# An expert kernel whose gate-times-gelu weights are formed by ScalarE, with VectorE only spreading the gates

## The chip, the core and the metric

The kernel runs on one core of a Trainium2 chip. A core has five engines that work side by side, each through its own queue and in that queue's order: TensorE (PE in the profile) multiplies matrices, VectorE (DVE) does elementwise arithmetic and reductions, ScalarE (ACT) computes functions and copies with a scale, GpSimd (POOL) here only issues gathers, and SyncE (SP) issues plain loads. Data comes from HBM by DMA. The metric is the device time of one execution in microseconds (us), as the median of several.

## The reference

One layer of a decoder block: three token mixers, gates and an output projection, and then a mixture of experts (PEER) in which each of 1024 tokens picks 16 experts in each of 8 heads out of 16384. The change touches only this last part:

```python
top_s, pos = lax.top_k(cand, PEER_TOPK)
idx = jnp.take_along_axis(cand_idx, pos, axis=-1)
gate = jax.nn.softmax(top_s, axis=-1)

def chunk(args):
    hc, ic, gc = args
    act = jax.nn.gelu(jnp.einsum('chkd,cd->chk', u[ic], hc).astype(jnp.float32), approximate=False)
    w = (gc * act).astype(h.dtype)
    return jnp.einsum('chk,chkd->cd', w, v[ic])
```

For each token, 128 rows of `u` are gathered and multiplied with the token's row, gelu of the product times the gate is the expert's weight, and the weighted sum of 128 rows of `v` is the output.

## The kernel before

The 1024 tokens are eight blocks of 128. Two blocks (`DENSE`, line 31) are computed against all 16384 experts with plain matmuls. The other six go by gathers, and these are the **sets** of the change. A set (`g`, 32 to a block, 192 in all) is four tokens with their 128 experts, in four gathers of 128 rows of `u` and four of `v`, 512 KB each. Partition p of a gather belongs to token p // 32 of the set.

`Experts.step` (line 1133) is one gather, i = 0 to 3 within the set. It does in this order: at i = 0 it takes the set's tokens `hb`, spread over the partitions (`spread_rows`, line 1080: two matmuls on PE into `pb`, two copies on ScalarE into `hb`; written two gathers ahead, at i = 2 of the set before); then it runs what is due of earlier sets (`run_behind`, line 1148); issues the gather of `v` (line 1097 by `fetch`); and on VectorE multiplies the gathered `u` with `hb` and sums over the row (line 1151) into column i of `parts`. After i = 3 the rest of the set is put in `behind`, in three parts that run one gather apart, each at the `run_behind` of the next set's gathers:

1. at the next set's i = 0: `gelu`, one ScalarE instruction on `parts` (128 x 4), into `gel`. ScalarE's other functions need another table, so most gelus are framed by two table loads.
2. at i = 1: `weights`, two VectorE instructions: `gel` times the gates `gT` (line 1165), and its product with the constant `spread` (line 1166), which puts each weight in its token's column of a 128 x 32 matrix, four of them in `wz`.
3. at i = 2: `sums` (line 1177), 16 matmuls (32 in the profile) that multiply `wz` with the four `v` into `po`. VectorE adds `po` to the output row after every eighth set.

Gathered rows live in rings of buffers: five for `u` and six for `v` (`UP, VP`, line 44). A gather of `u` waits until the dot product has read its buffer, a gather of `v` until the sums have; both stand in one queue on GpSimd. `wz`, `gel`, `parts` and `hb` come from a pool with two buffers each (line 82).

The sets run beside all other work, the **filler**: attention and projections of the three token groups (2, 3 and 3 blocks; the sets begin once the first group's experts are chosen), then the dense blocks. A planner in the loop at the end of the kernel (lines 1428 to 1433) interleaves the two in the order of writing by its own estimates of matrix and DMA time. Line 90 then fixes ScalarE's order: its instructions stand in its queue as they are written. On all other engines a scheduler of the framework orders the instructions, by the place at which they are written and by a model of when their inputs are ready. So a step that is written later on ScalarE moves there by exactly that, and the others' queues are rearranged around it.

The names of tiles in the profile are those of the code; `bank` is a PSUM tile of the filler, `big` and `wide` are activations, `w` weights, `e` a projection's result on its way, `sc` expert scores, `sp` a bfloat16 copy of the normalised tokens on its way to DRAM (`b3d`).

Of the kernel before, what the change touches and what calls it, by code (L numbers as in the profile page):

```python
# [7 lines left out]
F32 = mybir.dt.float32  # L8
# [3 lines left out]
AF = mybir.ActivationFunctionType  # L12
# [65 lines left out]
def block_kernel(ctx: ExitStack, tc: tile.TileContext, io):  # L78
    nc = tc.nc
    pool = lambda name, bufs, **kw: ctx.enter_context(tc.tile_pool(name=name, bufs=bufs, **kw))  # L80
    gat = pool("gat", 1)
    gw = pool("gw", 2)
# [10 lines left out]
    spread = keep.tile([128, QB, 32], BF, bufs=1)  # L93
# [29 lines left out]
    def actf(out, in_, f, **kw):  # L123
        s = SETS.get(f)
        if s and table[0] != s:
            nc.scalar.preload_act_table_set(s)  # L126
            table[0] = s
        nc.scalar.activation(out, in_, f, **kw)  # L128
# [929 lines left out]
    def rows_of(n, c):  # L1058
        b3 = gw.tile([96, D], BF, name="b3")
        nc.sync.dma_start(b3, b3d[n, c].rearrange("s t d -> (s t) d"))  # L1060
        return b3

    def quarters(dram_tile, c):

        return [dram_tile[32 * c:32 * c + 32, 256 * k:256 * k + 256] for k in range(4)]

    class Experts:
# [65 lines left out]
        def step(self):  # L1133

            self.supply()
            n, gT, box, g, i, ap = self.todo.pop(0)
            c, jj = divmod(g, QB)
            if i == 0:
                if jj == 4:
                    row = box["row"] = gw.tile([128, 256], F32, name="row", bufs=1)  # L1140
                    for k, src in enumerate(quarters(xres[n], c)):
                        nc.sync.dma_start(row[32 * k:32 * k + 32], src)
                    if c < 3:
                        box["b"] = rows_of(n, c + 1)
                self.spread_rows(n, box, g)
                self.hb = self.hbs.pop((n, g))
                self.parts = gw.tile([128, 4], F32, name="parts")
            self.run_behind()
            self.fetch("v", ap)
            u = self.us.pop(0)  # L1150
            nc.vector.scalar_tensor_tensor(u, u, 1.0, self.hb, op0=OP.mult, op1=OP.mult,  # L1151
                                           accum_out=self.parts[:, i:i + 1])
            if i == 2 and self.todo[1:]:
                m, _, near, h, j, _ = self.todo[1]
                if j == 0:
                    self.spread_rows(m, near, h)
            if i == 3:
                ge = gw.tile([128, 4], F32, name="gel")
                wz = gw.tile([128, 4, 32], F32, name="wz")

                def gelu(ge=ge, parts=self.parts):
                    actf(ge, parts, AF.Gelu)

                def weights(ge=ge, wz=wz):
                    nc.vector.tensor_mul(ge, ge, gT[:, c, jj, :])
                    nc.vector.tensor_mul(wz, ge[:, :, None].to_broadcast([128, 4, 32]),
                                         spread[:, jj, None, :].to_broadcast([128, 4, 32]))

                def sums(i, wz=wz, box=box):
                    if "po" not in box:  # L1170
                        box["po"] = pg.tile([128, 512], F32, name="po")
                    po = box["po"]
                    v = self.vs.pop(0)

                    h = 256 * (c % 2)
                    for k in range(4):
                        nc.tensor.matmul(po[32 * k:32 * k + 32, h:h + 256], wz[:, i, :],  # L1177
                                         v[:, 256 * k:256 * k + 256], start=jj == 0 and i == 0,
                                         stop=jj == QB - 1 and i == 3, skip_group_check=True)
                    if jj == QB - 1 and i == 3:  # L1180
                        row = box["row"]
                        nc.vector.tensor_add(row, row, po[:, h:h + 256])
                        for k, dst in enumerate(quarters(io["out"][n], c)):
                            nc.scalar.dma_start(dst, row[32 * k:32 * k + 32])
                self.behind.append([gelu, weights, lambda: [sums(x) for x in range(4)]])
            return g == 31 and i == 3

        def flush(self):
# [236 lines left out]
    while done < NT - ND or filler[0] is not None:  # L1425
# [11 lines left out]
        else:  # L1437
# [3 lines left out]
            c, m = cost[0], moved[0]  # L1441
# [55 lines left out]
```

## Time and profile before

| | |
|---|---|
| median of 3 runs | 3561.07 us (3557.21 to 3573.94) |
| the profiled execution's own time | 3568.14 us |
| its span, first to last instruction | 3566.4 us |
| granted TensorE clock, mean | 0.937 |
| time without sets (first group) | to about 490 us |
| filler ends, sets alone from there | about 3404 us |

The profile is of one execution. Busy time and idle time are given by engine; the waits name the instruction that waited and what released it; PEld is the load of a matmul's stationary matrix, which runs beside PE. A wait on PEld and one on PE can be the same idle time, so the two are not added up.

### The profile page before, as it was taken

Reading aid. Unit: us, or ns where it says so; the run is one execution under the profiler, and the core shown is the slowest. Engines: PE = TensorE matmul, PEld = TensorE weight load, DVE = VectorE, ACT = ScalarE, POOL = GpSimd, SP = SyncE. Lnnn points to the kernel's source line nnn. Section 1 sums busy time; section 2 is a strip of 40 time slices with the busy share of each in tenths; the row PEclk is TensorE's granted clock in tenths of the full one; section 3 lists DMA queues with packets and bytes.
Section 4 is the critical chain, followed back from the end, with each engine's and each line's share of the span. In section 5 each row is a group of like instructions: output and inputs, shape, how many; then the busy total and the mean of one; then the engine's idle time right before and its main releaser. Section 6 shows DMA issues by size and latency. Waiting matters only on the chain.

```text
span 3566.4 us, 60764 instructions
## 1 busy us (share of the span) xinstructions
PE 3196.1 (90%) x22802; PEld 2361.1 (66%) x22802; DVE 2341.1 (66%) x5985; ACT 1353.6 (38%) x2729; POOL 1778.4 (50%) x1544
## 2 busy tenths in 40 slices
PE   6999989989999889999998999776779999999954
PEld 6889856656555766666565657654568888888710
DVE  5444487565545468996656665798867677777654
ACT  4443135554411214656544222222324444444410
POOL 0000036656566556666555655566745444544476
PEclk9989989999999999999999999897899999999965
DMA  4425669999899999999998999989999999999999
GB/s 151 139 84 182 206 221 334 333 348 331 313 406 392 403 363 347 337 331 350 331 355 296 391 391 400 350 325 348 393 386 393 365 382 384 394 379 372 344 383 362
DMA packets 346430, 1185.54 MB, mean 332 GB/s; under 512 B 38744, under 2 KB 80216, under 8 KB 326680
## 3 DMA queue, kind: packets, MB, share of 16 engines
q0 software_dynamic: 221184, 805.40, 59.6%
q1 hardware_dynamic: 102672, 337.95, 26.0%
q10 hardware_dynamic: 22280, 38.31, 2.8%
q8 instruction: 180, 2.95, 0.3%
q14 instruction: 114, 0.93, 0.1%
HBM read 1142.18 MB, written 39.32 MB: 331 GB/s over the span
## 4 chain that ended last, share of the span: by engine, by line
PE 61%; DMA 15%; DVE 13%; issue 5%; ACT 3%; POOL 2%; ACTq 0%; SPq 0%; POOLq 0%; DVEq 0%
PE bank L117 32%; PE bank L1195 20%; PE po L1177 7%; DMA u<-in_u,iT 7%; DVE u L1151 3%; DMA v<-in_v,iT 3%; PE pb L1090 1%; DMA b3d<-sp 1%; PE bank L121 1%; POOL v L1097 1%; POOL u L1097 1%; DMA g<-gd 1%; ACT L126 1%; DMA gd<-g 1%; ACT e L128 1%
## 5 line engine op out<-in xcount | busy, mean ns | idle before, releaser
L1097 POOL DMA_INDIRECT u<-in_u,iT x768 | 916.2, 1193 | 956.1 <-DVE i L865 489.6
L1097 POOL DMA_INDIRECT v<-in_v,iT x768 | 861.4, 1122 | 818.8 <-PE po L1177 646.0
L1151 DVE SCALAR_TENSOR_TENSOR u<-u,hb 128x1024 f32<-128x1024 f32 x768 | 926.7, 1222 | 440.1 <-ACT hb L128 256.3
L1177 PE MATMUL po<-v,wz 128*32 128x256 f32 x6144 | 444.8, 416 | 155.3 <-DMA v<-in_v,iT 88.6
L117 PE MATMUL bank<-wide,w 128*128 128x384 f32 x1536 | 519.6, 492 | 1.8 <-DMA w<-in_w_gate 1.8
L1177 PEld LDWEIGHTS po<-v,wz 128*32 128x32 f32 x6144 | 182.0, 115 | 375.0 <-DMA v<-in_v,iT 119.0
L117 PEld LDWEIGHTS bank<-wide,w 128*128 128x128 f32 x1536 | 292.3, 192 | 201.3 <-issue 6.8
L128 ACT ACTIVATE hb<-pb 128x512 f32<-128x512 f32 x384 | 208.2, 594 | 397.2 <-PE pb L1090 251.3
L117 PEld LDWEIGHTS bank<-w,wide 128*128 128x128 f32 x2304 | 263.0, 192 | 7.4 <-issue 2.2
L117 PE MATMUL bank<-w,wide 128*128 128x128 f32 x2304 | 265.3, 275 | 0.2 <-DMA w<-in_w_out 0.2
L1195 PE MATMUL bank<-hh,ul 128*128 128x256 f32 x848 | 240.0, 283 | 1.2 <-DVE ul L1275 1.2
L1195 PE MATMUL bank<-hh,uh 128*128 128x256 f32 x848 | 240.9, 284 | 0.0
L1195 PE MATMUL bank<-hl,uh 128*128 128x256 f32 x848 | 239.9, 283 | 0.0
L117 PE MATMUL bank<-big,w 128*128 128x256 f32 (+1 forms) x1280 | 235.6, 341 | 1.2 <-DMA w<-in_w_pq 1.2
L117 PEld LDWEIGHTS bank<-big,w 128*128 128x128 f32 x1280 | 208.3, 193 | 27.0 <-issue 3.0
L128 ACT ACTIVATE e<-bank 128x512 f32<-128x512 f32 (+2 forms) x208 | 109.6, 527 | 306.8 <-PE bank L117 301.2
L1195 PE MATMUL bank<-vh,wh 128*128 128x512 f32 x512 | 202.9, 403 | 3.1 <-ACT vh L128 3.1
L1195 PE MATMUL bank<-vl,wh 128*128 128x512 f32 x512 | 201.9, 394 | 2.1 <-DVE vl L1275 2.0
L1195 PE MATMUL bank<-vh,wl 128*128 128x512 f32 x512 | 199.4, 389 | 0.0
L126 ACT ACT_TABLE_LOAD x144 | 184.8, 1283 | 21.7 <-issue 8.8
L128 ACT ACTIVATE w<-bank 128x256 f32<-128x256 f32 x128 | 49.3, 385 | 366.9 <-PE bank L1195 285.5
L1275 DVE TENSOR_TENSOR vl<-vr,vh 128x1024 fp32r<-128x1024 f32 x128 | 156.9, 1226 | 32.7 <-ACT vh L128 32.7
(297 smaller groups left out, 5659.9 us busy)
## 6 DMA issues: line engine op xcount, KB each, us to landing
ur<-in_uT SPq DMA_DIRECT2D x64, 1024.0 KB
vr<-in_vd SPq DMA_DIRECT2D x64, 1024.0 KB
w<-in_w_in SPq DMA_DIRECT2D x102, 512.0 KB
w<-in_w_gate SPq DMA_DIRECT2D x72, 512.0 KB
w<-in_w_pq SPq DMA_DIRECT2D x48, 512.0 KB
g<-gd SPq DMA_DIRECT2D x16, 1024.0 KB
w<-in_w_o SPq DMA_DIRECT2D x48, 256.0 KB
w<-in_w_out SPq DMA_DIRECT2D x24, 512.0 KB
```

The costliest lines, as they stand in the source:

```text
L117: nc.tensor.matmul(out, lhsT, rhs, **kw)
L121: nc.tensor.transpose(out, in_, ident)
L126: nc.scalar.preload_act_table_set(s)
L128: nc.scalar.activation(out, in_, f, **kw)
L1090: nc.tensor.matmul(pb, which[:, jj].rearrange("p q s -> p (q s)"), box["b3"][:, f], start=True, stop=True)
L1097: nc.gpsimd.indirect_dma_start(out=t, out_offset=None, in_=io[kind], in_offset=bass.IndirectOffsetOnAxis(ap=ap, axis=0))
L1151: nc.vector.scalar_tensor_tensor(u, u, 1.0, self.hb, op0=OP.mult, op1=OP.mult, accum_out=self.parts[:, i:i + 1])
L1177: nc.tensor.matmul(po[32 * k:32 * k + 32, h:h + 256], wz[:, i, :], v[:, 256 * k:256 * k + 256], start=jj == 0 and i == 0, stop=jj == QB - ...
L1195: nc.tensor.matmul(out, lhsT, rhs, **kw)
L1275: nc.vector.tensor_sub(lo, r[:, x], hi)
```

## The change

```diff
@@ step, i == 0
                 self.parts = gw.tile([128, 4], F32, name="parts")
+                self.wz = gw.tile([128, 4, 32], F32, name="wz")
+                nc.vector.tensor_mul(self.wz, gT[:, c, jj, :, None].to_broadcast([128, 4, 32]),
+                                     spread[:, jj, None, :].to_broadcast([128, 4, 32]))
             self.run_behind()
@@ step, i == 3
                 ge = gw.tile([128, 4], F32, name="gel")
-                wz = gw.tile([128, 4, 32], F32, name="wz")
-
-                def gelu(ge=ge, parts=self.parts):
+                wz = self.wz
+
+                def weights(ge=ge, wz=wz, parts=self.parts):
                     actf(ge, parts, AF.Gelu)
-
-                def weights(ge=ge, wz=wz):
-                    nc.vector.tensor_mul(ge, ge, gT[:, c, jj, :])
-                    nc.vector.tensor_mul(wz, ge[:, :, None].to_broadcast([128, 4, 32]),
-                                         spread[:, jj, None, :].to_broadcast([128, 4, 32]))
+                    for x in range(4):
+                        actf(wz[:, x, :], wz[:, x, :], AF.Copy, scale=ge[:, x:x + 1])
...
-                self.behind.append([gelu, weights, lambda: [sums(x) for x in range(4)]])
+                self.behind.append([None, weights, lambda: [sums(x) for x in range(4)]])
```

VectorE now spreads the gates into `wz` when the set begins, before its dot products. The gelu is written one gather later, at the next set's i = 1, and right behind it ScalarE scales the four 128 x 32 parts of `wz` by the four columns of `gel`, which it reads as a scale for each partition. The sums are still written at i = 2. The two buffers of `wz` are now taken at a set's beginning, when the sums of the set two before may still read one of them; 162 of the 192 spreads carry a wait for those matmuls. Nearly every sum (634 of 768 groups of four matmuls) waits for its own quarter of `wz` alone.

The first place is in the second token group, where the experts of that group are being scored (1250 us in the trace; there `big` is the normalised tokens or their projections). On ScalarE, `e`, `sc`, `wide` and `sc` are copies of scores out of PSUM. Before:

```order
L128 ACTIVATE gel<-parts 128x4
L128 ACTIVATE e<-bank 128x384
L128 ACTIVATE sc<-bank 128x128
L128 ACTIVATE wide<-bank 128x128
L128 ACTIVATE sc<-bank 128x128
L853 DMA b3d<-sp 4x32x1024
L128 ACTIVATE hb<-pb 128x512 x2
```

and of the change:

```order
L128 ACTIVATE e<-bank 128x384
L128 ACTIVATE sc<-bank 128x128
L128 ACTIVATE wide<-bank 128x128
L128 ACTIVATE sc<-bank 128x128
L853 DMA b3d<-sp 4x32x1024
L128 ACTIVATE gel<-parts 128x4
L128 ACTIVATE wz<-wz,gel 128x32 x4
L128 ACTIVATE hb<-pb 128x512 x2
```

The gelu went behind four copies that wait for PE, and ahead of the `hb` of a later set, which now also has the four scalings in front. Over the program, gelu stands at the same place among ScalarE's other work in 88 sets and 1 to 15 instructions later in 104; all else on ScalarE keeps its order.

On VectorE at the same set, before (`MAX` to `MATCH_REPLACE` build the lists of best scores, `s` and `i`):

```order
L855 CAST sp<-wide 128x1024
L1151 SCALAR_TENSOR_TENSOR u,parts<-u,hb 128x1024 x4
L864 MAX s_10061<-sc 128x8
L864 MAX s_11450<-wide 128x8
L865 MAX_INDEX i_10062<-s_10061,sc 128x8
L928 TENSOR_TENSOR sc<-s_10061 128x48
L866 MATCH_REPLACE sc<-s_10061,sc 128x128
L867 MAX s_10061<-sc 128x8
L1165 TENSOR_TENSOR gel<-gel,gT 128x4
L868 MAX_INDEX i_10062<-s_10061,sc 128x8
L928 TENSOR_TENSOR sc<-s_10061 128x64
L1166 TENSOR_TENSOR wz<-gel,spread 128x128
```

and of the change, a set that begins there:

```order
L1149 TENSOR_TENSOR wz<-gT,spread 128x128
L1154 SCALAR_TENSOR_TENSOR u,parts<-u,hb 128x1024 x4
L864 MAX s_10207<-sc 128x8
L864 MAX s_11630<-wide 128x8
L865 MAX_INDEX i_10208<-s_10207,sc 128x8
L866 MATCH_REPLACE sc<-s_10207,sc 128x128
```

The product that stood behind a cast, four dot products and eight rows of list work now stands ahead of the dot products, and nothing on VectorE lies between gelu and the sums any more.

On PE at the same set, before:

```order
L117 MATMUL bank<-big,w 128x256 x8
L117 MATMUL bank<-big,w 128x128 x8
L117 MATMUL bank<-big,e 128x128 x3
L1177 MATMUL po<-v,wz 32x256 x16
L1090 LDWEIGHTS which
L1090 MATMUL pb<-b_9420,which 128x512
```

and of the change, from the second half of the spreading (the products with `e` stand ahead of it):

```order
L1090 LDWEIGHTS which
L1090 MATMUL pb<-b_9548,which 128x512
L117 MATMUL bank<-big,w 128x256 x4
L1177 MATMUL po<-v,wz 32x256 x16
L117 MATMUL bank<-big,w 128x256 x4
L117 MATMUL bank<-big,w 128x128 x8
```

The sums moved behind the two spreading matmuls of a later set and behind half of the next projection. From about the 146th set on the sums stand at the same place among PE's other work as before.

The third place is in the dense stage (2784 us), ScalarE again. Here `w` is the gelu of the dense products on its way out of PSUM, and `wh`, `vh`, `uh` are the high halves of weights. Before:

```order
L128 ACTIVATE vh<-vr 128x1024
L128 ACTIVATE gel<-parts 128x4
L128 ACTIVATE uh<-ur 128x1024
L128 ACTIVATE w<-bank 128x256
L128 ACTIVATE wh<-w 128x256
L128 ACTIVATE vh<-vr 128x1024
```

and of the change:

```order
L128 ACTIVATE uh<-ur 128x1024
L128 ACTIVATE w<-bank 128x256
L128 ACTIVATE gel<-parts 128x4
L128 ACTIVATE wz<-wz,gel 128x32 x4
L128 ACTIVATE wh<-w 128x256
L128 ACTIVATE vh<-vr 128x1024
```

The gelu of the set went behind two more dense products (`w`), and stands between the second `w` and its `wh`.

## The prediction

> **What bounds the kernel now.** I read the page first, then busy time by stretches, then the waits.
>
> ```profile
> span 3566.4 us, 60764 instructions
> PE 3196.1 (90%) x22802; PEld 2361.1 (66%) x22802; DVE 2341.1 (66%) x5985; ACT 1353.6 (38%) x2729; POOL 1778.4 (50%) x1544
> 490.00:2300.00 1810.00, 1687.83 (x11972) 1138.62 (x11971) 1180.17 (x3191) 724.28 (x1461) 1086.52 (x967) 0.96 0.95 355
> 2300.00:2620.00 320.00, 239.63 (x1743) 174.46 (x1745) 282.04 (x1027) 85.27 (x265) 207.12 (x172) 0.88 0.94 358
> 2620.00:3400.00 780.00, 760.36 (x5399) 642.57 (x5392) 543.61 (x852) 348.32 (x578) 365.47 (x283) 0.99 0.98 376
> 3400.00:3567.00 167.00, 79.05 (x545) 16.79 (x543) 82.77 (x157) 18.00 (x46) 118.46 (x115) 0.54 0.96 378
> ```
>
> A stretch's row gives its length, the busy time of PE, PEld, DVE, ACT and POOL, the granted clock, the DMA engines' share and GB/s. PE is busy 93% in the groups' stretch (490 to 2300 us) and 97% in the dense one, with the DMA engines at 95 and 98%. Only the passage between them (2300 to 2620) leaves PE 80 us, and the tail is the gathers' alone. PE has 122 us of idle time to win back in the groups' stretch, 80 in the passage and 20 in the dense stretch. What of it hangs on the sets is in the waits from 490 to 2600 us (total, times, longest):
>
> ```profile
> PEld po L1177 <- DVE wz L1166: 73.4, 48, 11.2
> PE po L1177 <- DVE wz L1166: 53.0, 26, 11.0
> DVE gel L1165 <- ACT gel L128: 50.5, 26, 6.2
> ACT gel L128 <- DVE u L1151: 15.4, 6, 5.9
> PEld bank L117 <- ACT e L128: 14.3, 28, 1.2
> PEld bank L117 <- ACT g L128: 11.4, 7, 4.0
> PEld bank L117 <- DVE sp L520: 20.3, 11, 5.4
> POOL v L1097 <- PE po L1177: 369.0, 183, 11.8
> ```
>
> PE stood 53.0 us before the sums because VectorE had not made `wz`. ScalarE almost never waited for the dot products (15.4 us): these run far ahead, and gelu comes late because its queue does. In the tail both differ:
>
> ```profile
> ACT gel L128 <- DVE u L1151: 123.9, 14, 11.3
> PE po L1177 <- DMA v<-in_v,iT: 66.9, 50, 2.4
> 3552.87 7.75 DMA v<-in_v,iT
> 3560.66 1.13 PE po L1177 x8
> ```
>
> There the last `v` to land sets the end, 7.75 us after its issue, so a weight made some tenths later or earlier costs nothing; I take the tail's length as unchanged.
>
> **The change part by part.** *VectorE leaves the path from gelu to the sums.* One of the 26 waits, on the second group's scoring:
>
> ```profile
> 1250.47 0.20 ACT L128 ACTIVATE gel<-parts 128x4 f32<-128x4 f32 x1
> 1249.69 5.40 PE L117 MATMUL bank<-big,w 128*128 128x256 f32 x32
> 1252.10 0.69 DVE L855 CAST sp<-wide 128x1024 bf16<-128x1024 f32 x1 [7.83 <-DMA b3d<-sp]
> 1254.93 0.83 PE L117 MATMUL bank<-big,e 128*128 128x128 f32 x6
> 1256.13 0.28 ACT L128 ACTIVATE sc<-bank 128x128 f32<-128x128 f32 x1
> 1258.66 0.14 DVE L1165 TENSOR_TENSOR gel<-gel,gT 128x4 f32<-128x4 f32 x1
> 1259.18 0.28 DVE L1166 TENSOR_TENSOR wz<-gel,spread 128x128 f32<-128x128 f32 x1
> 1259.52 2.79 PE L1177 MATMUL po<-v,wz 128*32 128x256 f32 x24 [3.76 <-DVE wz L1166]
> ```
>
> Gelu was done at 1250.67, but VectorE had sat 7.83 us on a buffer still being stored, then had four dot products and list work ahead; `wz` came 8.8 us after gelu and PE lost 3.76. This goes with the change. **Removed: 53 us.** It can be no more than the 73.4 of the PEld row, which is partly the same time, and no less than nothing.
>
> *Gelu and the scalings stand later on ScalarE.* At this place the gelu now follows the second `sc`, so it starts at 1256.13 + 0.28 = 1256.41, 5.9 us later, though that copy itself moves with PE. With the durations below, the first quarter of `wz` is there at about 1257.0. PE meanwhile has, after the products with `e` (to 1255.76), two spreading matmuls (0.6, as in the row at 2773 us further down) and half of the 256-wide part of a projection: that part is two thirds of the 5.40 us, half of it 1.8. PE is at the sums at 1258.2, and the margin is 1.2 us. So here the wait vanishes, but the margin is thin.
>
> I made the same count for the 140 sets between 490 and 2600: PE's work, in the new order and with the groups' mean durations, from the matmul for which ScalarE last waits ahead of the gelu to the sums, less ScalarE's work from there to the first quarter. Made for the old order too, and set against the trace, it says by how much it errs at each set, and I carried that over. This is an estimate. Its mean margin falls from 3.3 to 1.9 us; sets below zero go from 11 (11 us, gelu itself late) to 35, with 41 us of waiting. The 11 are already in the 53. **Added: 41 us** of new waits for ScalarE. The bounds: nothing, if PE's own delays cover them, and 100 us, if every quarter is a microsecond later than counted (72 sets below zero). I stay at the count itself, since for the old order its middle error was 0.3 us or less in each of seven stretches.
>
> In the dense stretch the gelu moves up to ten microseconds:
>
> ```profile
> 2773.41 0.60 PE L1090 MATMUL pb<-b,which 96*128 96x512 bf16 x2
> 2784.07 0.19 ACT L128 ACTIVATE gel<-parts 128x4 f32<-128x4 f32 x1
> 2793.78 0.38 ACT L128 ACTIVATE w<-bank 128x256 f32<-128x256 f32 x1 [3.03 <-PE bank L1195]
> 2795.06 1.93 PE L1177 MATMUL po<-v,wz 128*32 128x256 f32 x32
> ```
>
> It now follows that `w` (done at 2794.16), so the first quarter is there at about 2794.7 and the sums, at 2795.06, do not wait; the other three come about every 0.2 us, and PE needs 1.93 / 4 = 0.48 for each. Cost nothing, but by 0.4 us.
>
> *Four scalings on ScalarE.* No row shows a 128 x 32 copy from SBUF with a scale from a tile. The nearest:
>
> ```profile
> L128 ACT ACTIVATE gel<-parts 128x4 f32<-128x4 f32 x192 | 39.2, 204 | 147.3 <-DVE u L1151 145.4 <-issue 1.0
> L128 ACT ACTIVATE hb<-pb 128x512 f32<-128x512 f32 x384 | 208.2, 594 | 397.2 <-PE pb L1090 251.3 <-issue 65.5 <-DVE u L1151 16.2
> L128 ACT ACTIVATE st<-st 128x1 f32<-128x1 f32 x16 | 3.2, 203 | 0.5
> L128 ACT ACTIVATE st<-st,eps 128x1 f32<-128x1 f32 x8 | 2.4, 295 | 0.2
> 2274.29 1.08 ACT L128 ACTIVATE hb<-pb 128x512 f32<-128x512 f32 x2 [3.98 <-issue]
> ```
>
> From 4 to 512 elements it is 390 ns more, 0.77 ns each, so 32 cost 204 + 22; a tile as operand adds 295 - 203 = 92: 318 ns. Two `hb` took 1.08 rather than 1.19, so each starts 0.1 early: four make 4 x 318 - 3 x 100 = 0.97 us, an estimate; at least 4 x 0.20 and at most 4 x 0.59. Over 192 sets that is 187 us more on ScalarE, 724 of 1810 us busy in the groups' stretch. Its cover is that PE seldom waits for ScalarE there: 14.3 + 11.4 us in 28 + 7 waits. If each grew by 0.97, it would be 34 us; if none, nothing. I take a quarter, **8 us**, since most of these waits do not follow a gelu at once.
>
> *VectorE.* It loses the product with the gates and no longer waits for gelu:
>
> ```profile
> L1165 DVE TENSOR_TENSOR gel<-gel,gT x192: 139/155/214, 512.0 to 3555.9; 128x4 f32<-128x4 f32 x192
> L1166 DVE TENSOR_TENSOR wz<-gel,spread x192: 270/284/324, 512.2 to 3556.2; 128x128 f32<-128x128 f32 x192
> ```
>
> 192 x 155 ns = 30 us of work and the 50.5 us of waiting. The spread stays at 284 ns, only earlier. PE's waits for VectorE's filler (`sp` 20.3 us) are the most it can return; I take **6 us** saved.
>
> *The new wait of the spread.* It waits for the sums of the set two before, and behind it stand that set's four dot products, then POOL, whose gathers of `u` need their buffers. At the least nothing; at the most the 162 carried waits last one block of sums, 1.93 us each, 313 us on VectorE. Its cover is the lead of the dot products, for which gelu waited only 15.4 us; **3 us** of it I let reach PE. With the cover gone, it would be the whole of it.
>
> Sums that come a microsecond later free the `v` buffers later; POOL already waits 369 us for them, and PE's order, not the gathers, sets when they are used, so I price that at nothing.
>
> **The sum:** -53 + 41 + 8 - 6 + 3 = -7 us. The profiled execution took 3568.1 us (its span and 1.7 around it), so 3561 in its own terms; it lies 7 above the median of the runs, 3561.07, and against that the forecast is **3554 us**.
>
> **The rivals.** *The gain whole:* the new order leaves ScalarE enough time, and only the 11 us remain in which gelu itself was late: -53 + 11 - 6 = -48, 3513 us. For it speaks that the order was made with ScalarE's new queue in view, against it the margin of 1.9 us.
>
> *The gelu too late:* written a gather later, it reaches the sums' turn after PE, at the sets of the groups' stretch. If the quarters come a microsecond later than counted, 100 us of waits replace the 53: -53 + 100 + 8 - 6 + 3 = +52, 3613 us. At half a microsecond the waits are 67 us and the sum is +19, 3580; that is the point from which it is slower. The thin margins speak for it, the good fit for the old order against.
>
> *ScalarE too full:* it is at its fullest in the first and fourth stretch, with 42 sets:
>
> ```profile
> 490.00:800.00 310.00, 285.74 (x1989) 192.90 (x1987) 210.45 (x580) 160.08 (x280) 194.50 (x170) 0.95 0.92 342
> 1400.00:1700.00 300.00, 285.82 (x2100) 194.09 (x2099) 253.34 (x804) 187.05 (x300) 197.88 (x173) 0.98 0.93 339
> ```
>
> 187.05 of 300 us are busy, and PE takes ScalarE's results there. If all 42 x 0.97 = 41 us came through in place of the 8, the sum is +26, 3587 us. The Trainium skill, "ScalarE: Activation LUTs", section "Rules for kernel authors", says to put multiplications on VectorE and not on ScalarE; by that rule alone this rival would win, while the trace, with VectorE the fuller of the two, bears it out only in part.
>
> *The change does not take VectorE off the path:* the spread, waiting for old sums, holds VectorE as the product did, and all stays as it was, 3561 us.
>
> **How the numbers follow.** The forecast and the last rival end within 0.5% of 3561 (18 us, about what a measurement of this kernel can tell from no change): 0.36 and 0.05. The gain whole or most of it: 0.31. Too late: 0.20. Too full: 0.08. So faster 0.31, same 0.41, slower 0.28. The range takes in the whole gain, at 3513, and the late gelu up to 0.8 us, +35 or so: 3512 to 3596, which leaves out about 0.2.
>
> **What would show it.** In the waits from 490 to 2600 us, PE before the sums should name ScalarE's `wz` and come to 30 to 55 us; under 20 is the gain whole, over 70 the late gelu. The scalings' row should show about 320 ns, PE's waits for `e` and `g` stay under 40 us, and VectorE's spread wait for `po` under 60 us. If the tail, from the end of the filler, is not 163 us long within 5, or the passage from 2300 to 2620 changes by over 20 us, the forecast misses for a reason that it does not hold: the scheduler's other order.

## The result and the profile after

| | before | changed kernel |
|---|---|---|
| median of 6 runs each, in turn on one chip | 3571.22 us (3557.21 to 3574.48) | 3608.57 us (3601.59 to 3610.45) |
| ratio, 95% interval | | 1.0109 (1.0087 to 1.0130) |
| the profiled execution's own time; span | 3568.14; 3566.4 us | 3602.05; 3599.9 us |
| filler ends; sets alone from there | 3401.0; 165.3 us | 3437.3; 162.6 us |

The changed kernel is 1.1% slower and lies 12.6 us above the range of the forecast; 10 us of that is the kernel before, which took 3571 us here where the forecast started from 3561. Every ratio here is against runs of the kernel before in the same job, on the same chip.

The page after, span and engines:

```profile
span 3599.9 us, 61952 instructions
PE 3211.1 (89%) x22802; PEld 2365.0 (66%) x22802; DVE 2323.9 (65%) x5793; ACT 1526.3 (42%) x3493; POOL 1796.6 (50%) x1544
```

ScalarE has 173 us more to do and VectorE 17 less. PE, whose instructions are the same, is busy 15 us longer. Busy time by stretch (length; PE, PEld, DVE, ACT, POOL; granted clock; DMA share; GB/s):

```profile
490.00:2300.00 1810.00, 1677.56 (x11920) 1129.20 (x11921) 1154.01 (x3015) 824.83 (x1918) 1081.05 (x958) 0.96 0.94 351
2300.00:2620.00 320.00, 232.94 (x1668) 167.20 (x1667) 272.67 (x1026) 98.64 (x333) 204.21 (x165) 0.84 0.93 350
2620.00:3440.00 820.00, 793.24 (x5579) 664.21 (x5578) 571.12 (x866) 395.52 (x761) 396.62 (x302) 0.98 0.97 372
3440.00:3600.00 160.00, 78.16 (x522) 15.50 (x522) 75.41 (x134) 29.97 (x101) 113.87 (x113) 0.53 0.98 389
```

In the groups' stretch PE does 10 us less in the same 1810, in the passage 7 less, and the passage's clock is 0.84 after 0.88. The waits from 490 to 2600 us (total, times, longest):

```profile
PEld po L1177 <- ACT wz L128: 74.8, 79, 15.6
PE po L1177 <- ACT wz L128: 44.5, 20, 15.1
PE po L1177 <- DMA v<-in_v,iT: 25.9, 18, 5.7
PE pb L1090 <- ACT hb L128: 13.6, 5, 9.1
PEld bank L117 <- ACT e L128: 37.0, 44, 3.0
PE bank L117 <- ACT e L128: 21.2, 25, 2.5
PEld bank L117 <- DVE sp L520: 25.9, 23, 4.7
DVE wz L1149 <- PE po L1177: 107.6, 46, 7.2
POOL v L1097 <- PE po L1177: 419.3, 201, 12.5
```

and of the kernel before, beside the rows that the forecast showed:

```profile
PE po L1177 <- DMA v<-in_v,iT: 21.7, 13, 4.9
PE pb L1090 <- ACT hb L128: 19.7, 5, 9.3
PE bank L117 <- ACT e L128: 3.1, 7, 0.7
```

VectorE's `wz` is gone from PE's waits, and ScalarE's `wz` stands there with 44.5 us where it had 53.0. PE's waits for the filler's `e` have grown (PE from 3.1 to 21.2, PEld from 14.3 to 37.0), those for `hb` before the spreading matmuls have shrunk, and VectorE's 107.6 us before the early spread are new. The four scalings are what they were taken for (by line and shape: busy us, mean ns, idle before):

```profile
L128 ACT ACTIVATE wz<-wz,gel 128x32 f32<-128x32 f32 x768 | 184.0, 310 | 6.5
```

The set at 1250 us that the forecast worked through stands in the timeline after (start, length, engine, instruction, idle before) at 1267:

```profile
1267.02 0.28 ACT L128 ACTIVATE sc<-bank 128x128 f32<-128x128 f32 x1
1267.32 0.21 ACT L128 ACTIVATE gel<-parts 128x4 f32<-128x4 f32 x1
1267.56 0.96 ACT L128 ACTIVATE wz<-wz,gel 128x32 f32<-128x32 f32 x4
1268.43 1.06 ACT L128 ACTIVATE hb<-pb 128x512 f32<-128x512 f32 x2
1268.74 1.93 PE L1177 MATMUL po<-v,wz 128*32 128x256 f32 x32
```

The first quarter of `wz` is there at 1267.87, and the half projection ahead of the sums keeps PE until the sums begin at 1268.74: margin 0.9 us where 1.2 was forecast, and PE does not wait. But `hb`, behind the scalings, is now made while the sums run. To see the whole, I added up every gap of PE (with PEld, over 20 ns) up to the end of the filler, by where PE stood and what ended the gap, from the trace:

| us | before | after | forecast of the difference |
|---|---|---|---|
| before the sums (`wz`, gathered `v`) | 77.2 | 70.7 | -53 + 41 |
| in the filler, for ScalarE | 60.4 | 71.6 | +8 |
| in the filler, for VectorE | 72.0 | 80.0 | -6 + 3 |
| in the filler, for nothing that shows | 55.6 | 65.2 | none |
| other | 3.8 | 4.3 | none |
| all idle | 269.0 | 291.8 | |
| the rest: PE or PEld busy, and the 12.7 and 12.5 us before PE's first instruction | 3132.0 | 3145.5 | none |

The span is 33.5 us longer: 22.8 of idle time, 13.5 of longer work of PE and PEld at a clock of 0.933 after 0.937, and 2.7 back in the tail. The ends of matmuls are modelled, so the border between idle and busy is not sharp.

### The profile page after: what moved, and what is told of

It is laid out like the page before. It is cut to its first block, busy times and chain, and to the rows that moved or that the text cites. A ratio compares the mean times of both kernels' runs of the same rounds, so it can differ in the third digit from the quotient of the medians.

```text
span 3599.9 us, 61952 instructions
## 1 busy us (share of the span) xinstructions
PE 3211.1 (89%) x22802; PEld 2365.0 (66%) x22802; DVE 2323.9 (65%) x5793; ACT 1526.3 (42%) x3493; POOL 1796.6 (50%) x1544
## 4 chain that ended last, share of the span: by engine, by line
PE 61%; DVE 15%; DMA 13%; ACT 5%; issue 3%; POOL 1%; ACTq 1%; SPq 0%; POOLq 0%; DVEq 0%
PE bank L117 32%; PE bank L1195 20%; PE po L1177 7%; DMA u<-in_u,iT 5%; DVE u L1154 4%; DMA v<-in_v,iT 3%; PE pb L1090 1%; DMA b3d<-sp 1%; ACT L126 1%; DMA gd<-g 1%; ACT e L128 1%; PE bank L121 1%; DMA g<-gd 1%; ACT rs L128 1%; POOL v L1097 1%
## 5 line engine op out<-in xcount | busy, mean ns | idle before, releaser
L1097 POOL DMA_INDIRECT v<-in_v,iT x768 | 882.1, 1149 | 871.8 <-PE po L1177 712.1
L117 PEld LDWEIGHTS bank<-wide,w 128*128 128x128 f32 x1536 | 291.8, 192 | 205.5 <-issue 13.0
L128 ACT ACTIVATE wz<-wz,gel 128x32 f32<-128x32 f32 x768 | 184.0, 310 | 6.5
```

The lines of the kernel that those rows point to most:

```text
L117: nc.tensor.matmul(out, lhsT, rhs, **kw)
L1097: nc.gpsimd.indirect_dma_start(out=t, out_offset=None, in_=io[kind], in_offset=bass.IndirectOffsetOnAxis(ap=ap, axis=0))
```

## The experiments

They ran in six jobs, on chips on which the kernel before takes 3567 to 3569 us (the third and fourth job) and on chips on which it takes 3714 to 3745 (the others). The changed kernel itself gave 1.0092 on the one kind and 1.0061 on the other, so ratios of different kinds are compared to no better than 0.3%.

**First job: the pieces of the edit.**

Gelu and scalings back at the next set's i = 0:

```diff
-                self.behind.append([None, weights, lambda: [sums(x) for x in range(4)]])
+                self.behind.append([weights, None, lambda: [sums(x) for x in range(4)]])
```

> Gelu and the four scalings together, but where gelu stood before the change (one gather earlier); the spread stays at the set's beginning. If the loss is the later place of gelu, it goes: PE's waits for wz before the sums fall under 20 us between 490 and 2600 us and the time is 1 to 1.5% under that of before (about 3525). If the loss is ScalarE's added work (0.97 us a set in front of the attention's e), PE's waits for e stay near the 58 us of the changed kernel (37.0 + 21.2) and the time is 0.5 to 1% above before. If it is the spread's wait for its buffer (107.6 us on VectorE in the changed kernel), it shrinks with the sums' lateness to about half, and the time lies between.

Measured: 3773.09 us, **1.0091** (1.0060 to 1.0122).

The kernel before with only its gelu moved one gather later, ahead of both VectorE products:

```diff
-                self.behind.append([gelu, weights, lambda: [sums(x) for x in range(4)]])
+                self.behind.append([None, weights, lambda: [sums(x) for x in range(4)]])
...
-                def gelu(ge=ge, parts=self.parts):
+                def weights(ge=ge, wz=wz, parts=self.parts):
                     actf(ge, parts, AF.Gelu)
-
-                def weights(ge=ge, wz=wz):
                     nc.vector.tensor_mul(ge, ge, gT[:, c, jj, :])
```

> The kernel before with its gelu one gather later, nothing else: both VectorE products stay, ScalarE makes no scalings. If the later place is the loss: slower than before by 1% or more, since the chain through VectorE now starts later too, with PE's waits for wz at 90 us or more. If ScalarE's added work is the loss: PE's waits for e stay near the 14 us of before, and the time is within 0.5% of before. If the buffer is the loss: within 0.5% as well, since here wz is taken late as before.

Measured: 3824.25 us, **1.0219** (1.0183 to 1.0255).

The changed kernel with the spread written after the set's fourth dot product:

```diff
@@ i == 3
-                wz = self.wz
+                wz = gw.tile([128, 4, 32], F32, name="wz")
+                nc.vector.tensor_mul(wz, gT[:, c, jj, :, None].to_broadcast([128, 4, 32]),
+                                     spread[:, jj, None, :].to_broadcast([128, 4, 32]))
```

> The changed kernel with the spread of the gates written after the set's fourth dot product in place of its beginning, so that its buffer has long been read. If the wait for the buffer is the loss: VectorE's waits of the spread for po fall from 107.6 us to under 20, and the time returns to within 0.5% of before. If it is the place of gelu or ScalarE's work: PE's waits for wz (44.5) and for e (58) stay, and the time stays 0.8 to 1.3% above before.

Measured: 3774.14 us, **1.0096** (1.0061 to 1.0130).

The changed kernel with four more small copies on ScalarE behind the scalings:

```diff
+                    for _ in range(4):
+                        actf(ge, ge, AF.Copy)
```

> The changed kernel with four more ScalarE copies of 128 x 4 behind the scalings of each set (gel onto itself, read by nobody): about 0.8 us more on ScalarE for each of 192 sets, without making any sum later by itself. If ScalarE's work is the loss: PE's waits for e grow by another 15 to 30 us and the time by 0.5 to 1% over the changed kernel. If it is the place or the buffer: the time stays within 0.3% of the changed kernel's.

Measured: 3799.81 us, **1.0163** (1.0131 to 1.0194).

The later place by itself, with VectorE still behind it, is the worst of all, and with VectorE's part off the path more than half of that is not lost. But the place is not the whole loss of the changed kernel: with gelu back in its old place and the scalings kept, the sums stand within 2 matmuls of where they stood before, on the mean, and the first run is still as slow as the third, in which they stand as in the changed kernel. The third run does not test the buffer: VectorE's waits before its spread come to 172 us (all releasers together, 490 to 2600 us) and not to under 20. The fourth run lies 0.67% over the third, with 158 us of copies more and the spread at another place.

**Second job: the changed kernel again, and ways around ScalarE.** The changed kernel itself:

> The changed kernel itself, so that it stands on one chip with the others: 1.0109 [1.0087, 1.013] before; 1.009 to 1.013 expected by every theory.

Measured: 3741.83 us, **1.0061** (1.0036 to 1.0087).

Gelu at i = 0 and one product on VectorE at i = 1 in place of the scalings:

```diff
-                    for x in range(4):
-                        actf(wz[:, x, :], wz[:, x, :], AF.Copy, scale=ge[:, x:x + 1])
+                    nc.vector.tensor_mul(wz, wz, ge[:, :, None].to_broadcast([128, 4, 32]))
```

> Spread at the set's beginning as in the change, gelu where it was before the change, and in place of the four scalings one VectorE product of wz with the broadcast gelu, where the two VectorE products were. ScalarE has exactly the work of before. If ScalarE's added work is the loss: back to within 0.5% of before, and PE's waits for e back to about 14 us. If the early spread (its wait for the buffer, or the order it makes) is the loss: 0.5 to 1.5% above before.

Measured: 3731.57 us, **1.0048** (1.0030 to 1.0066). With no new work on ScalarE, PE's waits for `e` are still 39.2 us on PEld here (45.9 in the changed kernel of this job), so on this kind of chip the 14.3 us of the trace before are no base to compare with.

Gelu at i = 0, the scalings on ScalarE at i = 1:

```diff
-                self.behind.append([None, weights, lambda: [sums(x) for x in range(4)]])
+                self.behind.append([gelu, weights, lambda: [sums(x) for x in range(4)]])
```

> Gelu where it was before the change, the four scalings one gather later as in the change: the table loads lie as before, the scalings on ScalarE as in the change. The run with both at the early place lost 0.9%. If the scalings' time on ScalarE is the loss: again 0.7 to 1.2%. If the place of the table loads is: within 0.5% of before.

Measured: 3737.01 us, **1.0064** (1.0041 to 1.0086). Table loads frame fewer gelus than the section on the kernel before says: its trace has 144 loads (`ACT_TABLE_LOAD`) for 192 gelus, and that of the change 140.

The kernel before with four small copies on ScalarE behind each gelu:

```diff
                     actf(ge, parts, AF.Gelu)
+                    for _ in range(4):
+                        actf(parts, parts, AF.Copy)
```

> The kernel before with four ScalarE copies of 128 x 4 written behind each gelu (parts onto itself, read by nobody after the gelu): about 0.8 us more on ScalarE a set, as the scalings are, and nothing that the sums wait for. If ScalarE's added work is the loss: 0.5 to 1% above before, PE's waits for e at 30 us or more. If not: within 0.4%.

Measured: 3728.65 us, **1.0040** (1.0017 to 1.0063). So ScalarE's load alone, 158 us, with the sums in their old place in all but 15 of the first 140 sets, costs 0.4%, some 15 us. The rule of the Trainium skill ("ScalarE: Activation LUTs", "Rules for kernel authors") that multiplications belong on VectorE is neither borne out nor refuted: one product on VectorE gave 1.0048, four scalings on ScalarE 1.0064 with gelu in the same place, and the intervals overlap. The two differ in more than the engine: with the scalings the sums stand later on PE, by some 5 matmuls on the mean.

**Third job: wait, load and buffer apart.** The kernel before against itself:

> The kernel before against itself on this chip, which gives the size of what two loads of the same program differ by, and a trace of it here. Every theory: ratio 1.000, within 0.25%; PE's waits for VectorE's wz between 490 and 2600 us near 55 us, none of VectorE's wz for PE. If it differs from 1 by more than 0.3%, then ratios of half a per cent in the other runs say little.

Measured: 3567.64 us, **0.9995** (0.9984 to 1.0007). Half a per cent can be read.

The changed kernel without its scalings:

```diff
-                    for x in range(4):
-                        actf(wz[:, x, :], wz[:, x, :], AF.Copy, scale=ge[:, x:x + 1])
```

> The changed kernel without the four scalings (the sums take the mask times the gates alone, the gelu is made and not used): neither ScalarE's 184 us of copies nor the sums' wait for them is left; VectorE's early spread and its wait for the wz buffer are. If the new wait on ScalarE (44 us) and its load are the loss, PE gains about 44 us and 15 to 20 more on waits for e: ratio to before 0.985 to 0.992. If the loss comes from the early spread that waits for the buffer on VectorE (155 us of waits on this chip), the ratio stays within 0.3% of the changed kernel's 1.006.

Measured: 3575.61 us, **1.0022** (1.0010 to 1.0035).

The same with five small copies in the scalings' place:

```diff
+                    for _ in range(5):
+                        actf(ge, ge, AF.Copy)
```

> The run without scalings, and in their place behind the gelu five small copies of the gelu's 128x4 onto itself (206 ns each, 1.03 us a set against the scalings' 0.96): ScalarE's load is back, the sums' wait for ScalarE is not. If the load is what costs, it lies 0.4 to 0.6% above the run without scalings; if the wait costs and not the load, it lies within 0.2% of it.

Measured: 3604.65 us, **1.0091** (1.0073 to 1.0109). The waits of the run without scalings, from 490 to 2600 us (the 155 us in its expectation are of the second job's chip):

```profile
DVE wz L1149 <- PE po L1175: 117.4, 65, 7.1
POOL v L1097 <- PE po L1175: 223.7, 142, 12.4
PE po L1175 <- DMA v<-in_v,iT: 94.3, 53, 5.4
PE bank L117 <- ACT e L128: 2.7, 5, 1.3
```

and of the run with the copies, with the row of their group:

```profile
POOL v L1097 <- PE po L1177: 215.0, 126, 12.7
PE po L1177 <- DMA v<-in_v,iT: 108.6, 54, 6.0
PE bank L117 <- ACT e L128: 10.9, 11, 2.5
L128 ACT ACTIVATE gel<-gel 128x4 f32<-128x4 f32 x960 | 197.1, 205 | 30.6
```

In both, weights that are ready early let the scheduler place the sums earlier on PE, by 33 and 38 matmuls of the filler on the mean of the first 140 sets, and put filler between them: 18 and 21 matmuls of it stand within a set's sums, 3 in the kernel before. There PE waits 94 and 109 us for `v` where the kernel before waited for `wz`. In neither does a sum wait for ScalarE; the 197 us of copies cost 0.69%, 25 us.

The run without scalings also shows where gained idle time can go. Against the trace of the kernel before in this job, PE and PEld are idle 33 us less and busy 25 us longer (the profiled execution is the fastest of its kernel). The sums of the kernel before, and of this run (busy us, mean ns, idle before):

```profile
L1177 PE MATMUL po<-v,wz 128*32 128x256 f32 x6144 | 443.2, 416 | 151.8 <-DMA v<-in_v,iT 80.7 <-DVE wz L1166 66.3 <-issue 2.2
L1175 PE MATMUL po<-v,wz 128*32 128x256 f32 x6144 | 484.6, 417 | 181.6 <-DMA v<-in_v,iT 160.2 <-DVE u L1154 10.0 <-DVE row L1180 6.6
```

Each matmul is as long as before, but cut up as they are fewer of them overlap, and the same 6144 take 41 us more of PE's time.

The kernel before with the `wz` buffer taken at the set's beginning by a small product:

```diff
+                self.wz = gw.tile([128, 4, 32], F32, name="wz")
+                nc.vector.tensor_mul(self.wz[:, 0, 0:4], gT[:, c, jj, :], spread[:, jj, 0:4])
```

> The kernel before, with the wz buffer taken at the set's beginning by one small product on VectorE (128x4, about 150 ns), so that VectorE waits there for the sums of two sets ago, as in the changed kernel; the gelu, the gate product and the whole wz product stay where they were. If that wait on VectorE is the part of the loss that the run with one product showed (1.0048), the ratio is 1.004 to 1.006. If it costs nothing because VectorE is ahead there, 1.000 to 1.002.

Measured: 3575.58 us, **1.0012** (1.0001 to 1.0023), with this wait of VectorE and PE's before the sums:

```profile
DVE wz L1149 <- PE po L1179: 110.1, 64, 6.5
PE po L1179 <- DVE wz L1168: 56.9, 25, 11.6
```

110 us of VectorE's waiting, as much as in the changed kernel, cost 4 us of time, and PE's wait before the sums stays near the 57.5 us of the kernel before in this job: most of VectorE's waiting is covered by its lead.

**Fourth job: the counterpart.** The changed kernel again:

> The changed kernel itself, beside the next two, so that its parts can be added up. Ratio 1.009 to 1.011 if load and wait are as the result had them on a chip of the same time before; lower where the chip is slower.

Measured: 3603.82 us, **1.0092** (1.0072 to 1.0112).

One column scaled in place of four quarters:

```diff
-                    for x in range(4):
-                        actf(wz[:, x, :], wz[:, x, :], AF.Copy, scale=ge[:, x:x + 1])
+                    actf(wz[:, 0, 0:1], wz[:, 0, 0:1], AF.Copy, scale=ge[:, 0:1])
```

> The changed kernel with one copy of one column of the wz buffer (about 200 ns) in the place of the four scalings (so the sums take the mask times the gates, but for that column): the sums still wait for ScalarE behind the gelu, ScalarE's load is cut from 184 to about 40 us. If the wait for ScalarE is the loss, 1.006 to 1.010. If the wait only takes the place of the wait for the gathered v, as the run without scalings (1.0022) suggests, and the load is the loss, 1.002 to 1.004.

Measured: 3599.00 us, **1.0083** (1.0060 to 1.0107).

Two small copies in place of five:

```diff
-                    for _ in range(5):
+                    for _ in range(2):
                         actf(ge, ge, AF.Copy)
```

> The changed kernel without the scalings and with two small copies of the gelu (206 ns each) in their place, where five gave 1.0091 and none 1.0022. If the loss follows ScalarE's load, 1.004 to 1.006; if only the fullest stretches count and the first copies are free, under 1.003.

Measured: 3589.17 us, **1.0050** (1.0033 to 1.0067).

So with the sums where the earlier weights put them, the loss goes with the dose: 1.0022, 1.0050, 1.0091 at 0, 2 and 5 copies a set (the second from this job, the others from the third). But the run with the wait and little load is as slow as the changed kernel, against what the theory of the load expected. Its waits and its copy:

```profile
PE po L1176 <- ACT wz L128: 45.3, 18, 13.5
PE po L1176 <- DMA v<-in_v,iT: 32.8, 16, 6.4
PE bank L117 <- ACT e L128: 11.7, 19, 1.8
L128 ACT ACTIVATE wz<-wz,gel 128x1 f32<-128x1 f32 x192 | 56.6, 295 | 6.4
```

It has 127 us less ScalarE work, and PE waits 10 us less for `e` than in the changed kernel (21.9 us in the run beside it); but then it waits for `v`, 32.8 us (27.1 beside). In these two kernels the sums stand at the same place among PE's work in 179 of the 192 sets: later than in the kernel before in 65 of the first 140 sets, earlier in 12, on the mean some 6 matmuls later. At this place of the sums 127 us of ScalarE's work are worth no more than 5 us by the medians, and the two intervals overlap.

**Fifth job: the priced wait taken away.** The kernel before, its sums fed from a constant tile:

```diff
-                        nc.tensor.matmul(po[...], wz[:, i, :],
+                        nc.tensor.matmul(po[...], iota[:, 0:32],
```

> The kernel before with every instruction in its place, but its sums take a constant 128x32 tile in place of wz (so the weights are left out of the output): PE waits before its sums for the gathered v alone. This is the 53 us of the prediction taken away by themselves. If they were there to be had, 0.985 to 0.990. If the gather of v stands right behind each of them, 0.998 to 1.002, with PE's waits for v between 490 and 2600 us grown from 16-22 to some 70 us or more.

Measured: 3679.69 us, **0.9904** (0.9882 to 0.9926).

The changed kernel likewise, without spread and scalings:

> The changed kernel with sums that take the same constant tile, and neither the scalings nor the early spread of the gates made (no weights at all; the gelu stays and is not used): neither chain, load, wait on ScalarE nor wait on VectorE for a buffer. If VectorE's early wait for the wz buffer is what kept the run without scalings from gaining (1.0022), this one comes out below 0.995. If the gathers bound the sums anyway, within 0.3% of 1.

Measured: 3671.10 us, **0.9894** (0.9875 to 0.9912). In the first of these two runs, from 490 to 2600 us, `wz` is gone and `v` has taken its place:

```profile
PE po L1177 <- DMA v<-in_v,iT: 87.2, 46, 6.2
POOL v L1097 <- PE po L1177: 221.0, 76, 14.3
```

Both gain about 1%, 34 and 43 us of 3714, the first at the edge of the gain that its expectation names. But the sums moved, by some 32 matmuls earlier as in the run without scalings, and PE does not wait less before them. There is no trace of the kernel before on this kind of chip; the nearest is its run with four copies behind each gelu, where the sums stand as before:

```profile
PE po L1179 <- DVE wz L1168: 65.9, 27, 12.6
PE po L1179 <- DMA v<-in_v,iT: 5.2, 5, 2.1
```

These 71 us became 87. By the count of gaps used above, the first run here has 24 us more before its sums than that run, and some 70 less in the filler; against the run with one product, which has no copies, it is 30 more and some 60 less. So the time was gained in the filler, with the sums moved, and not in the wait that was taken away.

**Sixth job: a third buffer.**

```diff
-    ones = const.tile([128, 128], F32)
-    nc.vector.memset(ones, 1.0)
+    one = const.tile([128, 1], F32)
+    nc.vector.memset(one, 1.0)
+    ones = one.to_broadcast([128, 128])
...
-                self.wz = gw.tile([128, 4, 32], F32, name="wz")
+                self.wz = gw.tile([128, 4, 32], F32, name="wz", bufs=3)
```

> The changed kernel with a third wz buffer (its 512 bytes a partition come from the 128x128 tile of ones, which becomes one column that is read broadcast, as the kernel does with its minus ones). The wait for a wz buffer on VectorE (103 to 117 us between 490 and 2600 us with two buffers) should be gone or below 20 us; the scalings' load and the sums' wait for ScalarE stay. If that wait on VectorE is what took the gain back (the runs 1.0022 without scalings against 0.9894 without the buffer too, 1.3 apart), the changed kernel's 1.0092 becomes 0.996 to 1.000. If it is hidden (the touch alone in the kernel before cost 0.0012), 1.007 to 1.010.

Measured: 3749.40 us, **1.0094** (1.0070 to 1.0118). The wait did not go. VectorE's waits before the spread with three buffers:

```profile
DVE wz L1150 <- PE pb L1091: 81.4, 24, 8.2
DVE wz L1150 <- PE bank L117: 28.0, 11, 5.8
DVE wz L1150 <- PE po L1178: 26.9, 9, 6.2
```

and with two, on the same kind of chip:

```profile
DVE wz L1149 <- PE pb L1090: 82.5, 24, 8.2
DVE wz L1149 <- PE po L1177: 38.9, 27, 6.2
DVE wz L1149 <- PE bank L117: 34.0, 19, 7.2
```

136 us against 155, or 167 against 180 with all other releasers. With two buffers the spread starts 1.1 us after the end of the sums of the set two before (the middle value of the first 140 sets); with three it starts 12 us before these end, 2.6 us after the sums of the set three before: the scheduler moved it a set ahead, to the next buffer that is not free. So this run says nothing on what the wait costs.

## Why the prediction was wrong

**VectorE off the path, -53.** The 53.0 us went, as said, and no PE instruction waits for VectorE's `wz`. That the time can fall at all without this wait is shown only where the sums are free of weights (0.9904), and there the gain was in the filler: before the sums PE waited for `v` (87.2 us).

**Gelu and scalings too late, +41.** Measured 44.5 us, inside the 30 to 55 that were to show it. One wait of 15.1 makes a third of it. The timeline of the changed kernel in the passage:

```profile
2399.77 0.60 PE L1090 MATMUL pb<-b,which 96*128 96x512 bf16 x2
2413.26 0.31 ACT L128 ACTIVATE s<-s 128x128 f32<-128x128 f32 x1 [11.37 <-DVE s L952]
2414.87 0.21 ACT L128 ACTIVATE gel<-parts 128x4 f32<-128x4 f32 x1
2415.11 0.96 ACT L128 ACTIVATE wz<-wz,gel 128x32 f32<-128x32 f32 x4
2415.48 1.08 PE L1177 MATMUL po<-v,wz 128*32 128x256 f32 x8 [15.11 <-ACT wz L128]
```

and of the kernel before:

```profile
2389.21 0.31 ACT L128 ACTIVATE s<-s 128x128 f32<-128x128 f32 x1 [6.93 <-DVE s L952]
2390.06 1.07 PE L1090 MATMUL pb<-b,which 96*128 96x512 bf16 x2 [9.29 <-ACT hb L128]
2391.80 0.20 ACT L128 ACTIVATE gel<-parts 128x4 f32<-128x4 f32 x1
2392.36 1.08 PE L1177 MATMUL po<-v,wz 128*32 128x256 f32 x8 [1.23 <-DVE wz L1166]
```

ScalarE's queue is fixed, and in it the gelu stands behind an exponential `s` of the gates, which waits for VectorE's list work. PE stood there before too, 9.29 + 1.23 us under two other names. So VectorE is still on the path at this place, through a filler's step in ScalarE's queue, and only 4.6 of the 15.1 us are new.

**Before the sums together** the forecast had -12 us and the gaps give -6.5: half the size, the right sign. That sums which come later free `v` later was priced at nothing. GpSimd's wait for the sums grew from 369.0 to 419.3 us, and PE's gaps before the sums for `v`, named or without a name, only from 21.2 to 23.6, so the price was right by this trace.

**The step that failed: all that stands outside the sums' waits, priced at +8 - 6 + 3 = +5 us.** The span grew by 33.5 us although 6.5 were gained before the sums, so the rest came to +40. A second pair of traces (the kernel before in the third job, the changed kernel in the fourth) gives +45. Term by term:

*The four scalings, +8.* Their length was right (310 ns and 0.96 us a set, for 318 and 0.97). What failed is the cover: "I take a quarter, 8 us, since most of these waits do not follow a gelu at once". The gaps for ScalarE in the filler grew by 11.2 us, and that is a net of two: some 17 us more in the filler's other matmuls, where the wait for `e` alone went from 3.4 to 21.2, and some 6 less before the spreading matmuls. PE's waits for `e` and `g` on PEld were to stay under 40 us and do (37.9), so that bound was too wide to show it. But a price by PE's waits on ScalarE is too small in itself. The traces of none and five copies (47 us apart, since the first is the fastest run of its kernel; the medians are 29 apart) show 14.9 us more of gaps in the filler for ScalarE, 16.3 more before the sums, where nearly all is the wait for `v`, and 14.6 of longer PE work. How much of the loss is the load of 184 us in the changed kernel itself is not shown: the copies cost 0.12 us for each us of load with the sums early, 0.09 in the kernel before, and 0.03 to 0.04 where the sums wait for ScalarE, which would be between some 5 and 23 us. The rival of the full ScalarE had this mechanism and the chance 0.08; its price, 41 us, is not shown by any run.

*VectorE freed, -6, and the spread's wait, +3.* PE's gaps for VectorE rose by 8.0 instead, 11 us from the forecast. VectorE waited 107.6 us for the buffer, not under 60; such a wait put into the kernel before cost 0.12% (0.01 to 0.23), about 4 us, near the 3. The 6 did not come.

*No term at all* stood for gaps that no releaser explains (+9.6 us; only +2.3 against the second trace of the kernel before) and for PE's own work (+13.5, at a clock of 0.933 after 0.937). A sum made of PE's waits alone leaves those 13.5 of the 33.5 us out. With the five copies that part grows by 14.6, and from one scaled column to four scalings, with the sums in place, by 16.7, so some of it belongs to the load.

The tail, 162.6 us, and the passage, 7 us less PE work, are inside their bounds.

**The other rivals.** The gain whole (3513) and the gelu too late (100 us of waits) fell by the 44.5 us; the one that VectorE stays on the path holds at one place only, that in the passage.

**Open.** What makes the +40 is not settled. Load without wait gives 1.0091, wait with little load 1.0083, and both together 1.0092: either is enough, and they do not add up. The sums stand at other places on PE in the first than in the two others, so these are not steps of one sum. What the wait costs by itself is not settled; with one scaled column it cannot be told from the later place of the sums. Open too is the 0.5% of the run with one product, which has neither the load nor later sums (1.0048), and why the early spread takes the gain back where the sums are placed alike (1.0022 with it, 0.9894 without weights at all, on different kinds of chip). No version tried computes the layer faster than the kernel before.

## What to carry over

Idle time of an engine does not by itself hide work that is added to its queue, when that queue is in order and feeds the engine that bounds the kernel: ScalarE was busy 38% of the span, and copies whose result nobody used still cost 0.09 to 0.12 us of the kernel's time for each us, only part of it in waits that name ScalarE. Where the sums already waited for ScalarE, more load cost little (0.03 to 0.04, unclear). Before a wait is priced as gain, take it away and see what is late next: with the 53 us of waits for weights gone, PE waited for the gathers, and the 34 us gained lay in the filler, with the sums moved. Where a scheduler orders the queues, an edit that frees a step also moves it, so look up its place in each trace before two kernels are compared as if one thing differed.

## What was not expected of the hardware

The same kernel takes 3567 to 3571 us on some chips and 3714 to 3745 on others. The mean granted clock of its runs was 0.935 to 0.936 in the third and fourth job and 0.923 to 0.927 in the first, second, fifth and sixth, a smaller difference than that of the times. The changed kernel gave 1.0092 (1.0072 to 1.0112) on the first kind and 1.0061 (1.0036 to 1.0087) on the second.

PE's busy time for the same 22802 matmuls does not follow the granted clock alone: 3195.6 us at 0.938 in the kernel before, 3211.1 at 0.933 in the changed kernel, 3223.4 at 0.936 without the scalings and 3237.7 at 0.931 with five copies. In the last two the sums are cut up, and they alone take 41 and 47 us more of it.
